# A two-layer trunk kernel: another order of token blocks in the mixers' last product, splits two blocks ahead, eight MLP pairs begun early, modulation slabs of two column blocks

## The chip, the cores and the metric

The kernel runs on one core of one Trainium2 chip. The metric is the time of one execution in device microseconds; the time shown is the median of several executions. The profiled execution is a single one with its own time. Engines are PE (matmul), PEld (its weight loads), DVE, ACT, POOL and SP, whose queue issues the DMAs.

## The reference

A batch of one sequence of 1024 tokens with 1024 features goes through two layers. Layer A has an mLSTM mixer, layer B multi-head latent attention; each is followed by an MLP with squared ReLU. A vector c gives shift, scale and gate for each part.

```python
for layer in range(DEPTH):                    # DEPTH = 2, layer 0 is A, layer 1 is B
    sh1, sc1, g1, sh2, sc2, g2 = split(silu(c) @ mod_w[layer] + mod_b[layer], 6)
    h = modulate(rms_norm(x, norm_g[layer, 0]), sh1, sc1)
    y = mlstm_mixer(h, ...) if layer == 0 else mla_mixer(h, ...)   # both end in "@ w_out"
    x = x + g1 * rms_norm(y, norm_g[layer, 1])
    h = modulate(rms_norm(x, norm_g[layer, 2]), sh2, sc2)
    y = square(relu(h @ ffn_w1[layer])) @ ffn_w2[layer]            # 1024 -> 4096 -> 1024
    x = x + g2 * rms_norm(y, norm_g[layer, 3])
```

`mlstm_mixer` projects h to q, k, v, an output gate and two scalar gates per head, runs a recurrence over chunks of 64 tokens, and multiplies the gated, normalised result by `w_out`. Everything is float32.

## The kernel before

**Matmuls.** Every operand is split into a rounded high half (a cast on ACT, L105, L438, L502, L546) and a low half (a subtraction on DVE, L106, L442, L504, L550). A product is three passes on PE: high by high (L155), low by high (L156) and high by low (L157). All engines work off their queues in order; the order within each queue is set by a scheduler when the kernel is built, from the program's order and its own costs. Work tiles come from a pool of 52 SBUF buffers (`U`), PSUM tiles from two of 1024 columns (`MM`) and four of 512 (`SM`).

**Start.** The first modulation (shift and scale of layer A) is needed as columns, one for each of 8 blocks k of 128 features. For each k a slab of `mod_w` (both column blocks of 128, all 1024 rows) is loaded in two tiles. DVE multiplies by the conditioning vector and adds over the 8 row blocks (`mod_sum`, L967 and L969, 8 operations of 128x256 for each k in two partial sums); POOL adds the two (L970); PE adds over the partitions by a matmul with a column of ones (`mod_col`, L976); DVE adds the bias (L978). Meanwhile ACT takes the sums of squares of the first four token blocks of x (L916), DVE the inverse roots (L164 to L172), ACT scales x (L920). `turned` transposes x on PE, ACT applies the modulation (L927) and casts, DVE makes the low half `hTl` (L106), and the projection of v and the gates (128x344 matmuls) follows for this k.

**Modulation of the rest.** `layer_mod(l, j)` is a list of steps: a DMA of 0.5 MB of `mod_w` (`modw`), a multiply-add of DVE (L263, L265) for each of 8 row blocks into `acc`, then transposes of `acc` on PE (L183) and a sum on DVE (L274). Other stages take steps from such lists: before, two after each of the last four blocks of v, six after each q or k head, and one after every third MLP product.

**End of a mixer.** For each token block, in the order `ORDER`, the gated result is turned and split (`gate_split` in layer A, `split` in layer B, one block ahead), multiplied by `w_out` (48 matmuls of 512 columns), normalised (ACT L178, DVE L164 to L172, L401, L402) and added to x (`mixer_out`). `h_norm` (L178, L492) prepares the MLP's input, `h_turn` transposes it (PE L183, ACT L457), `h_high` and `h_low` split it (L438, L442).

**MLP.** The up product of each of 16 pairs of column blocks is done in 7 products instead of 8. Products 1 and 2 need only the even token blocks; the other five need sums with the odd blocks (`odd_turn`, `odd_sums` L476 to L479, `odd_high`, `odd_low`). So `mlp_begin` starts with products 1 and 2 of the first `BEGUN` pairs. Their first weights come through `w_first` (DMA L499, ACT L502, DVE L504), the combined ones through `w_pair` (POOL L557 to L577, ACT L546, DVE L550). `up_product` adds each product to the pair's running sums (DVE L680, ACT L687, L683, L684).

Of the kernel before, what the change touches and what calls it, by code (L numbers as in the profile page):

```python
# [19 lines left out]
D = 1024  # L20
SEQ = 1024
P = 128
# [43 lines left out]
class Trunk:  # L66
# [356 lines left out]
    BEGUN = 6  # L423
# [204 lines left out]
    def mlp_begin(self, l, odd):  # L628
# [16 lines left out]
        up(2, 3, 5, 4)  # L645
        self.odd_turn(2, [odd.pop(5), odd.pop(7)])
        self.odd_low(0, "S1", "A22", "S4")
        up(3, 4, 5)
        self.odd_sums(2)
        self.w_step()  # L650
        up(4, 5)
        self.odd_high(2, "S2", "S3", "S1", "A22", "S4")
        self.odd_low(2, "S2", "S3")
        for _ in range(2):
            self.w_step()
        up(5)
        self.w_step()
        self.odd_low(2, "S1", "A22", "S4")
        self.w_step()

    def up_product(self, p, s):
# [7 lines left out]
        ps = st["ps"][:, (lo, hi)[s - 1]] if s in (1, 2) else self.SM()  # L669
# [49 lines left out]
    def mlp(self, l, done, extra, last=None):  # L719
# [43 lines left out]
        for p in range(NP):  # L763
            for o, s in enumerate((1, 2, 6, 7, 5, 4, 3)):
# [6 lines left out]
                if n % 3 == 0:  # L771
                    next(extra, None)
# [114 lines left out]
    def layer_a(self):  # L887
# [63 lines left out]
        def slab(k):  # L951

            w = T["mod_w"][0].rearrange("(i p) c -> p i c", p=P)
            us = [self.U("slab")[:, :D].rearrange("p (i s c) -> p i s c", i=4, s=2) for _ in range(2)]
            for j, u in enumerate(us):
                for s in range(2):
                    dma(out=u[:, :, s], in_=w[:, 4 * j : 4 * j + 4, s * D + k * P : s * D + (k + 1) * P])
            slabs.append([u.rearrange("p i s c -> p i (s c)") for u in us])

        def mod_sum(k):  # L960

            accs = [self.U("acc")[:, : 2 * P] for _ in range(2)]
            for i in range(KD):
                src, acc = slabs[k][i // 4][:, i % 4], accs[i % 2]
# [17 lines left out]
        def turned(k):  # L982

            ps = self.MM()
            mod_col(k, sums.pop(k), ps[:, 512:])
# [9 lines left out]
        load_xs(0, 2)  # L995
# [12 lines left out]
        turned(0)  # L1008
        for k in range(KD):
            if k < 4:  # L1010
                slab(k + 4)
            if k in (0, 2, 4):
# [819 lines left out]
```

## Time and profile before

| | |
|---|---|
| time, median of 3 executions | 2340.91 us (2340.1 to 2342.76) |
| profiled execution, its own time | 2336.43 us |
| its span from first to last instruction | 2334.7 us |
| mean granted clock of PE | 0.988 |
| busy: PE, PEld, DVE, ACT, POOL | 95%, 79%, 75%, 43%, 21% |

The own time is that of the execution which the rows below describe; the 1.7 us between it and the span lie before the first and after the last instruction. PE's share is an average: it is near 100% in most of the span and lower at the start (0 to 60 us), at about 100 to 110 us, and where a mixer passes into an MLP (464 to 645 us and 1610 to 1804 us). A granted clock of 1.00 stands for 2.4 GHz, one of 0.5 for 1.2 GHz.

### The profile page before, as it was taken

The page shows a single profiled execution, that of the slowest core. Times are in us where ns is not written, and L with a number is a line of the kernel's source. Part 1 is how long each engine was busy: PE and PEld are TensorE (multiplying, and loading weights), DVE is VectorE, ACT ScalarE, POOL GpSimd, SP SyncE. Part 2 cuts the span into 40 slices and gives each one's busy share as a digit, 9 for nine tenths or more (in the row PEclk, how much of TensorE's full clock was granted, in tenths as well). Part 3 has the DMA queues.
Part 4 walks back from the last instruction along what each step waited for, and adds up shares of the span by engine and source line. Part 5 has one row for each costly group of instructions (what it writes and reads, how often), then busy time and mean ns, then how long its engine had stood idle before and what let it go on. Part 6 is the DMA issues. An engine that isn't in the chain of part 4 may idle for free. (4 is left out here: it accounts for less than half of the span.)

```text
span 2334.7 us, 29139 instructions
## 1 busy us (share of the span) xinstructions
PE 2208.0 (95%) x10730; PEld 1833.8 (79%) x10730; DVE 1752.7 (75%) x2848; ACT 1007.7 (43%) x1637; POOL 480.7 (21%) x324
## 2 busy tenths in 40 slices
PE   5799999988999999999999999999889999999997
PEld 4798888866777777777798988987667888777776
DVE  6684676577888858788998676655777777588888
ACT  4421474563443464233344545544634444633321
POOL 1000110003433334231121000000034334333300
PEclk9999999999999999999999999999999999999999
DMA  9495343233665555454321000122346445544452
GB/s 272 142 322 201 100 73 99 91 109 127 221 226 189 190 180 160 119 167 146 102 88 44 17 17 15 46 73 81 109 156 220 152 149 189 172 131 140 142 174 99
DMA packets 304102, 318.09 MB, mean 136 GB/s; under 512 B 15976, under 2 KB 256216, under 8 KB 303960
## 3 DMA queue, kind: packets, MB, share of 16 engines
q1 hardware_dynamic: 303960, 316.23, 43.2%
q8 instruction: 84, 1.38, 0.2%
q14 instruction: 58, 0.48, 0.1%
HBM read 243.75 MB, written 72.43 MB: 135 GB/s over the span
## 5 line engine op out<-in xcount | busy, mean ns | idle before, releaser
L155 PE MATMUL mm<-whi,uh 128*128 128x512 f32 x688 | 273.1, 397 | 12.6 <-DVE y L760 10.7
L157 PE MATMUL mm<-whi,ul 128*128 128x512 f32 x688 | 271.2, 394 | 1.2 <-DVE ul L754 1.2
L156 PE MATMUL mm<-wlo,uh 128*128 128x512 f32 x688 | 271.1, 394 | 0.0
L577 POOL TENSOR_TENSOR tt<-raw,tt 128x512 f32<-128x512 f32 x60 | 118.0, 1967 | 668.7 <-DVE wlo L550 586.9
L760 DVE TENSOR_TENSOR y<-y,mm 128x1024 f32<-128x1024 f32 (+1 forms) x161 | 193.2, 1206 | 49.6 <-PE mm L157 49.4
L155 PE MATMUL sm<-hSh,whi 128*128 128x512 f32 x512 | 204.2, 399 | 11.3 <-DVE x L680 6.7
L157 PE MATMUL sm<-hSh,wlo 128*128 128x512 f32 x512 | 202.0, 396 | 2.2 <-DVE wlo L550 2.2
L156 PE MATMUL sm<-hSl,whi 128*128 128x512 f32 x512 | 202.5, 396 | 0.0
L550 DVE TENSOR_TENSOR wlo<-raw,whi 128x1024 fp32r<-128x1024 f32 x108 | 162.8, 1507 | 19.8 <-ACT whi L546 18.7
L754 DVE TENSOR_TENSOR ul<-u,uh 128x896 fp32r<-128x896 f32 (+1 forms) x120 | 151.0, 1289 | 32.0 <-ACT uh L748 24.4
L155 PEld LDWEIGHTS mm<-whi,uh 128*128 128x128 f32 x688 | 129.2, 188 | 49.2 <-DVE y L760 17.3
L680 DVE TENSOR_TENSOR x<-x,sm 128x512 f32<-128x512 f32 x192 | 127.8, 681 | 45.3 <-PE sm L157 41.9
L557 POOL TENSOR_TENSOR tt<-raw,raw 128x512 f32<-128x512 f32 x32 | 56.3, 1760 | 489.6 <-DVE hSl L442 461.5
L157 PEld LDWEIGHTS mm<-whi,ul 128*128 128x128 f32 x688 | 129.2, 188 | 32.4 <-DVE ul L754 2.1
L156 PEld LDWEIGHTS mm<-wlo,uh 128*128 128x128 f32 x688 | 129.2, 188 | 29.3
L748 ACT CAST uh<-u 128x896 fp32r<-128x896 f32 (+1 forms) x120 | 107.9, 945 | 84.8 <-PE mm L157 66.9
L265 DVE SCALAR_TENSOR_TENSOR acc<-modw,cact,acc 128x1024 f32<-128x1024 f32 x84 | 112.5, 1339 | 35.8 <-DMA modw<-in_mod_w_dram 29.1
L683 ACT ACTIVATE x<-x 128x1024 f32<-128x1024 f32 x64 | 67.7, 1058 | 155.2 <-DVE x L680 155.2
L582 ACT CAST w<-tt 128x512 fp32r<-128x512 f32 x60 | 37.2, 620 | 213.6 <-POOL tt L577 210.5
L155 PEld LDWEIGHTS sm<-hSh,whi 128*128 128x128 f32 x512 | 96.8, 189 | 37.9 <-DVE x L680 8.2
L546 ACT CAST whi<-raw 128x1024 fp32r<-128x1024 f32 x108 | 112.9, 1045 | 23.9 <-DVE wlo L550 10.2
L546 ACT CAST whi<-tt 128x1024 fp32r<-128x1024 f32 x60 | 62.9, 1048 | 136.9 <-issue 62.2
(404 smaller groups left out, 5991.7 us busy)
## 6 DMA issues: line engine op xcount, KB each, us to landing
raw<-in_ffn_w_dram SPq DMA_DIRECT2D x140, 512.0 KB
u<-us SPq DMA_DIRECT2D x112, 448.0 KB
us<-x SPq DMA_DIRECT2D x92, 512.0 KB
modw<-in_mod_w_dram SPq DMA_DIRECT2D x80, 512.0 KB
x<-xn SPq DMA_DIRECT2D x24, 512.0 KB
x<-x SPq DMA_DIRECT2D x24, 512.0 KB
x<-in_x_dram SPq DMA_DIRECT2D x16, 512.0 KB
slab<-in_mod_w_dram SPq DMA_DIRECT2D x32, 256.0 KB
```

What stands on the lines that cost most here:

```text
L155: mm(out, a[0], b[0], start=start, stop=False)
L156: mm(out, a[0], b[1], start=False, stop=False)
L157: mm(out, a[1], b[0], start=False, stop=stop)
L265: self.V.scalar_tensor_tensor(out=acc, in0=t, scalar=self.cact[:, k : k + 1], in1=acc, op0=ALU.mult, op1=ALU.add)
L546: S.copy(x[0], u)
L550: V.tensor_tensor(out=x[1], in0=u, in1=x[0].bitcast(F32), op=ALU.subtract)
L577: G.tensor_tensor(out=t1, in0=b21, in1=t2, op=ALU.subtract)
L680: V.tensor_tensor(out=dst, in0=src, in1=ps, op=ALU.add)
L683: S.activation(u, u, AF.Relu)
L748: S.copy(x[0], u)
L754: V.tensor_tensor(out=x[1], in0=u, in1=x[0].bitcast(F32), op=ALU.subtract)
L760: V.tensor_tensor(out=dst, in0=dst, in1=ps, op=ALU.add)
```

## The change

Five things are changed. The token blocks in both mixers' last product come in the order 0, 2, 4, 6, 1, 3, 5, 7. The turning and splitting of a block is issued two blocks ahead. Eight instead of six MLP pairs are begun, with `h_norm` for two blocks at a time, and two of the pairs (2 and 5) use `SM` tiles. The first modulation's slabs hold two column blocks (256 columns in one run of memory instead of 128), are all requested before other constants, and the sums for k = 0 and 1 are done by PE alone (L995, 8 matmuls of one column for each of shift and scale) instead of DVE, POOL and PE. `layer_mod(1, 2)` moves from the MLP of layer 0 to the end of the mixer's chunk loop, the steps after the blocks of v are dropped, q and k heads take seven instead of six, and MLP products two in five instead of one in three.

```diff
-    BEGUN = 6
+    BEGUN = 8
...
-    def h_norm(self, t):
-        x = self.mix[5].pop(t)
-        h = self.U("h")[:, :D]
-        self.S.activation(h, x, AF.Copy, scale=self.rms(x, D, h))
-        self.mix[6][t] = h
+    def h_norm(self, *ts):
+        xs = [self.mix[5].pop(t) for t in ts]
+        ssq = self.W("ssqs", [P, 4])
+        hs = [self.U("h")[:, :D] for _ in ts]
+        for i, (x, h) in enumerate(zip(xs, hs)):
+            self.S.activation(h, x, AF.Square, accum_out=ssq[:, i : i + 1])
+        r = self.rsqrt(ssq[:, : len(ts)], len(ts), 1.0 / D)
+        for i, (t, x, h) in enumerate(zip(ts, xs, hs)):
+            self.S.activation(h, x, AF.Copy, scale=r[:, i : i + 1])
+            self.mix[6][t] = h
...
-        up(0, 2, 4)
+        self.odd_sums(0)
+        up(0, 3, 4, 5)
+        self.h_norm(5, 7)
         self.odd_high(0, "S2", "S3")
-        self.h_norm(NT - 1)
-        up(1, 3)
-        self.w_step()
+        up(1, 4, 5, 6)
...
-            self.ups[p] = {"ps": self.MM(), "x": [self.U("x")[:, :1024], None]}
+            self.ups[p] = {"ps": None if p in (2, 5) else self.MM(), "x": [self.U("x")[:, :1024], None]}
...
-                if n % 3 == 0:
+                if n % 5 in (0, 2):
                     next(extra, None)
...
-            us = [self.U("slab")[:, :D].rearrange("p (i s c) -> p i s c", i=4, s=2) for _ in range(2)]
+            us = [self.U("slab")[:, :D].rearrange("p (i s c) -> p i s c", i=2, s=2) for _ in range(4)]
             for j, u in enumerate(us):
                 for s in range(2):
-                    dma(out=u[:, :, s], in_=w[:, 4 * j : 4 * j + 4, s * D + k * P : s * D + (k + 1) * P])
+                    dma(out=u[:, :, s], in_=w[:, 2 * j : 2 * j + 2, s * D + k * P : s * D + (k + 2) * P])
...
-                PE.matmul(ps[:, s : s + 1], acc[:, s * P : (s + 1) * P], self.ones[:, 0:1], start=True, stop=True)
+                if acc is not None:
+                    PE.matmul(ps[:, s : s + 1], acc[:, s], self.ones[:, 0:1], start=True, stop=True)
+                else:
+                    for i in range(KD):
+                        PE.matmul(ps[:, s : s + 1], slab_part(k, i)[:, s], self.cact[:, i : i + 1], start=i == 0, stop=i == KD - 1)
...
-        load_xs(2, 4)
+        for g in range(3):
+            slab(2 * g)
+            self._raw()
+        slab(6)
         normed(xs[:4], True)
-        slab(0)
-        self._raw()
-        mod_sum(0)
-        for k in range(1, 4):
-            slab(k)
-        for k in range(1, 4):
+        for k in range(2, 4):
             mod_sum(k)
...
-            for _ in range(2):
-                next(mods, None)
...
-                for _ in range(6):
+                for _ in range(7):
                     next(mods, None)
...
+        mods = self.layer_mod(1, 2)
+        self.early = 1
...
+                if j >= 2:
+                    next(mods, None)
+        finish(mods)
...
-    ORDER = (0, 1, 2, 3, 4, 6, 5, 7)
+    ORDER = (0, 2, 4, 6, 1, 3, 5, 7)
...
-        if n in (4, 6):
-            self.h_even(n - 4, [hs.pop(t) for t in ((0, 2) if n == 4 else (4, 6))])
-        elif n == 5:
+        if n in (3, 5):
+            j = n - 3
+            self.h_even(j, [hs.pop(t) for t in (2 * j, 2 * j + 2)])
+        elif n == NT - 1:
             self.odd_turn(0, [hs.pop(1), hs.pop(3)])
...
-        for p in {4: (0, 1), 5: (0, 2), 6: (0, 1, 3), 7: (1, 2)}.get(n, ()):
-            next(self.first[p], None)
+        for p in range(self.BEGUN):
+            if 0 <= n - 3 - p < 3:
+                next(self.first[p], None)
```

Three places show how instructions move. The first is DVE's queue at the start of the program. Before, the sums of the first slab (`acc_151`, `acc_152`) stand among the steps of the inverse root for x (`rst`, `rsy`):

```order
L170 TENSOR_TENSOR rst_126<-rsy_125,rsv_124 128x4
L171 TENSOR_TENSOR rst_126<-rst_126,rsy_125 128x4
L967 TENSOR_SCALAR acc_151<-slab_142,cact 128x256
L967 TENSOR_SCALAR acc_152<-slab_142,cact 128x256
L172 SCALAR_TENSOR_TENSOR rsy_125<-rst_126,rsy_125 128x4
L969 SCALAR_TENSOR_TENSOR acc_151<-slab_142,cact,acc_151 128x256
L969 SCALAR_TENSOR_TENSOR acc_152<-slab_142,cact,acc_152 128x256
L170 TENSOR_TENSOR rst_126<-rsy_125,rsv_124 128x4
L969 SCALAR_TENSOR_TENSOR acc_151<-slab_143,cact,acc_151 128x256
L969 SCALAR_TENSOR_TENSOR acc_152<-slab_143,cact,acc_152 128x256
L171 TENSOR_TENSOR rst_126<-rst_126,rsy_125 128x4
```

In the changed kernel DVE's queue after its first four small operations is this; `mm_219` and `mm_262` are PE's sums for k = 0 and 1, `acc_199` and `acc_209` DVE's for k = 2 and 3:

```order
L997 TENSOR_TENSOR modcol<-mm_219,bcols 128x2
L999 SCALAR_TENSOR_TENSOR modcol<-modcol,gcols 128x1
L982 TENSOR_SCALAR acc_199<-slab_130,cact 128x256 x2
L982 TENSOR_SCALAR acc_209<-slab_130,cact 128x256 x2
L984 SCALAR_TENSOR_TENSOR acc_199<-slab_131,cact,acc_199 128x256 x2
L984 SCALAR_TENSOR_TENSOR acc_209<-slab_131,cact,acc_209 128x256 x2
L997 TENSOR_TENSOR modcol<-mm_262,bcols 128x2
L984 SCALAR_TENSOR_TENSOR acc_199<-slab_132,cact,acc_199 128x256 x2
L984 SCALAR_TENSOR_TENSOR acc_209<-slab_132,cact,acc_209 128x256 x2
L999 SCALAR_TENSOR_TENSOR modcol<-modcol,gcols 128x1
L984 SCALAR_TENSOR_TENSOR acc_199<-slab_133,cact,acc_199 128x256 x2
L164 TENSOR_SCALAR rsv_181<-ssqs_172 128x4
```

DVE now takes PE's sum for k = 0 first, then 16 sums of the second slab, with PE's sum for k = 1 between them; the inverse root of x (from L164) starts at the last of these, where it began ahead of all sums before.

The second place is PE's queue in the first q head, where the columns of the next modulation are turned (`acc`, L183). Before, these two rows stand 27 rows behind the transpose of the positions (`posf`):

```order
L155 MATMUL sm_1012<-whi_552,hTh_785 128x344
L156 MATMUL sm_1012<-wlo_553,hTh_785 128x344
L157 MATMUL sm_1012<-whi_552,hTl_786 128x344
L183 MATMUL sm_1039<-ident,acc_855 128x128 x4
L183 MATMUL sm_1045<-ident,acc_855 128x128 x4
L155 MATMUL sm_1075<-whi_544,hTh_698 128x344
```

In the changed kernel the same place in the q head holds only a transpose of the gates, 75 rows behind `posf`:

```order
L156 MATMUL sm_1080<-wlo_553,hTh_785 128x344
L157 MATMUL sm_1080<-whi_552,hTl_786 128x344
L1211 MATMUL sm_1113<-ident,gate_1023 1x32
L155 MATMUL sm_1123<-whi_544,hTh_698 128x344
L156 MATMUL sm_1123<-wlo_545,hTh_698 128x344
```

and the turning of `acc` stands 164 rows behind `posf`:

```order
L155 MATMUL sm_1186<-whi_813,hTh_463 128x344
L156 MATMUL sm_1186<-wlo_814,hTh_463 128x344
L157 MATMUL sm_1186<-whi_813,hTl_464 128x344
L183 MATMUL sm_1213<-ident,acc_1014 128x128 x4
L183 MATMUL sm_1219<-ident,acc_1014 128x128 x4
L155 MATMUL sm_1225<-whi_801,hTh_243 128x344
L156 MATMUL sm_1225<-wlo_802,hTh_243 128x344
```

The turning of `acc` has moved back by 137 rows of PE's queue, and a small transpose for the gates, which DVE and ACT compute, now comes ahead of it.

The third place is ACT's queue at the end of layer A's mixer. `mm_4298` is the product of the last block but one; its sum of squares (L178) stands behind six of the eight copies of turned MLP input (L457, each row x2):

```order
L105 CAST aTh_4279<-gt_4281 128x512 x2
L492 ACTIVATE h_4259<-xn_4236,rsy_4263 128x1024
L457 ACTIVATE hr_4347<-sm_4348,modcol 128x256 x2
L457 ACTIVATE hr_4347<-sm_4355,modcol 128x256 x2
L457 ACTIVATE hr_4362<-sm_4363,modcol 128x256 x2
L178 ACTIVATE xn_4387,ssq_4388<-mm_4298 128x1024
L457 ACTIVATE hr_4362<-sm_4370,modcol 128x256 x2
L438 CAST hSh_4067<-hr_4347 128x2x256
```

In the changed kernel the sum of squares of the last block but one (`mm_4321`) and the work of `h_norm` (L497) stand ahead of the copies, and that of the last block (`mm_4395`) behind three of four:

```order
L507 CAST whi_4316<-raw_4167 128x1024
L178 ACTIVATE xn_4372,ssq_4373<-mm_4321 128x1024
L507 CAST whi_4390<-raw_4319 128x1024
L497 ACTIVATE h_4295<-xn_4147,rsy_4300 128x1024
L497 ACTIVATE h_4296<-xn_4277,rsy_4300 128x1024
L457 ACTIVATE hr_4444<-sm_4445,modcol 128x256 x2
L457 ACTIVATE hr_4444<-sm_4452,modcol 128x256 x2
L457 ACTIVATE hr_4459<-sm_4460,modcol 128x256 x2
L178 ACTIVATE xn_4474,ssq_4475<-mm_4395 128x1024
L507 CAST whi_4492<-raw_4393 128x1024
```

## Rows read from the trace of the kernel before

**Rows 1.** Windows: stretch, then busy us (x instructions) per engine, granted clock, DMA, GB/s.

```profile
0.00:60.00 60.00, 33.06 (x163) 29.15 (x163) 40.10 (x116) 26.83 (x37) 11.50 (x28) 0.97 0.93 265
290.00:464.00 174.00, 173.73 (x894) 146.57 (x893) 114.40 (x303) 96.89 (x213) 8.18 (x8) 1.00 0.33 84
464.00:561.00 97.00, 83.08 (x348) 64.43 (x347) 69.55 (x117) 51.66 (x84) 15.86 (x10) 0.93 0.37 108
561.00:645.00 84.00, 78.74 (x337) 61.66 (x336) 69.66 (x82) 38.32 (x40) 38.54 (x23) 1.00 0.63 208
1610.00:1725.00 115.00, 98.74 (x419) 77.64 (x418) 80.72 (x148) 64.97 (x108) 18.48 (x11) 0.94 0.35 103
1725.00:1804.00 79.00, 73.20 (x307) 57.27 (x306) 64.93 (x77) 36.20 (x38) 35.42 (x21) 0.98 0.66 215
1856.00:1914.00 58.00, 58.00 (x252) 46.98 (x251) 42.92 (x46) 25.15 (x27) 21.32 (x12) 1.00 0.45 148
```

**Rows 2.** PE in order of time, start: start us, us, line, operation, count.

```profile
18.64 1.01 PE L976 MATMUL mm<-ones,acc 128*128 128x1 f32 x4 [11.07 <-POOL acc L970]
...
31.23 1.50 PE L155 MATMUL sm<-whi,hTh 128*128 128x344 f32 x4
...
54.09 0.50 PE L976 MATMUL mm<-ones,acc 128*128 128x1 f32 x4
...
58.70 0.78 PE L157 MATMUL sm<-whi,hTl 128*128 128x344 f32 x4
```

**Rows 3.** DVE in order of time, start.

```profile
11.49 0.16 DVE L171 TENSOR_TENSOR rst<-rst,rsy 128x4 f32<-128x4 f32 x1
```

**Rows 4.** DVE groups, 0 to 60 us: count, busy us, mean ns, idle before.

```profile
L969 DVE SCALAR_TENSOR_TENSOR acc<-slab,cact,acc 128x256 f32<-128x256 f32 x48 | 21.8, 493 | 1.0 <-DVE rst L170 0.7 <-DMA slab<-in_mod_w_dram 0.3
L967 DVE TENSOR_SCALAR acc<-slab,cact 128x256 f32<-128x256 f32 x16 | 6.4, 433 | 3.7 <-DMA slab<-in_mod_w_dram 3.7
L106 DVE TENSOR_TENSOR hTl<-t,hTh 128x512 fp32r<-128x512 f32 x8 | 5.4, 680 | 4.0 <-ACT hTh L105 4.0
```

**Rows 5.** ACT in order of time, start.

```profile
9.70 1.06 ACT L916 ACTIVATE h<-x 128x1024 f32<-128x1024 f32 x1 [0.15 <-DMA x<-in_x_dram]
...
17.95 4.26 ACT L920 ACTIVATE x<-x,rsy 128x1024 f32<-128x1024 f32 x4 [7.10 <-DVE rsy L172]
...
23.59 0.62 ACT L105 CAST hTh<-t 128x512 fp32r<-128x512 f32 x1
```

**Rows 6.** DMA view, 8 to 45 us.

```profile
DMA packets 19893, 10.79 MB, mean 292 GB/s; under 512 B 1906, under 2 KB 19818, under 8 KB 19892
```

**Rows 7.** PE in order of time, 99 to 113 us.

```profile
110.47 1.94 PE L183 MATMUL sm<-ident,acc 128*128 128x128 f32 x8 [10.55 <-DVE acc L265]
...
112.78 0.49 PE L157 MATMUL sm<-whi,hTl 128*128 128x344 f32 x1
```

**Rows 8.** DVE in order of time, 99 to 113 us.

```profile
99.09 0.33 DVE L1169 TENSOR_SCALAR gate<-sm,gbias 32x128 f32<-32x128 f32 x1
...
112.79 0.27 DVE L1179 SCALAR_TENSOR_TENSOR gate<-gate 32x128 f32<-32x128 f32 x1
```

**Rows 9.** Waits of PE, 464 to 561 us: total, times, longest.

```profile
PE mm L157 <- DVE wlo L504: 4.2, 2, 2.2
PE mm L155 <- DVE xn L401: 3.4, 1, 3.4
```

**Rows 10.** ACT in order of time, 485 to 489 us.

```profile
485.14 2.84 ACT L457 ACTIVATE hr<-sm,modcol 128x256 f32<-128x256 f32 x6 [5.14 <-PE sm L183]
487.85 1.05 ACT L178 ACTIVATE xn<-mm 128x1024 f32<-128x1024 f32 x1
```

**Rows 11.** DVE groups, 464 to 645 us: count, busy us, mean ns, idle before.

```profile
L680 DVE TENSOR_TENSOR x<-x,sm 128x512 f32<-128x512 f32 x36 | 23.9, 678 | 8.8 <-PE sm L157 8.6
...
L504 DVE TENSOR_TENSOR wlo<-raw,whi 128x1024 fp32r<-128x1024 f32 x6 | 7.3, 1217 | 0.6 <-ACT whi L502 0.6
...
L442 DVE TENSOR_TENSOR hSl<-hs,hSh 128x512 fp32r<-128x512 f32 x8 | 5.1, 682 | 0.0
```

More of the change, by code (lines that the diff above doesn't have):

```diff
@@ L666, in up_product @@
         if p not in self.ups:
-            self.ups[p] = {"ps": self.MM(), "x": [self.U("x")[:, :1024], None]}
+            self.ups[p] = {"ps": None if p in (2, 5) else self.MM(), "x": [self.U("x")[:, :1024], None]}
         st = self.ups[p]
-        ps = st["ps"][:, (lo, hi)[s - 1]] if s in (1, 2) else self.SM()
+        ps = st["ps"][:, (lo, hi)[s - 1]] if s in (1, 2) and st["ps"] is not None else self.SM()
         w = self.w_take((0, p), s)
@@ L953, in slab, with slab_part @@
             w = T["mod_w"][0].rearrange("(i p) c -> p i c", p=P)
-            us = [self.U("slab")[:, :D].rearrange("p (i s c) -> p i s c", i=4, s=2) for _ in range(2)]
+            us = [self.U("slab")[:, :D].rearrange("p (i s c) -> p i s c", i=2, s=2) for _ in range(4)]
             for j, u in enumerate(us):
                 for s in range(2):
-                    dma(out=u[:, :, s], in_=w[:, 4 * j : 4 * j + 4, s * D + k * P : s * D + (k + 1) * P])
-            slabs.append([u.rearrange("p i s c -> p i (s c)") for u in us])
+                    dma(out=u[:, :, s], in_=w[:, 2 * j : 2 * j + 2, s * D + k * P : s * D + (k + 2) * P])
+            slabs.append(us)
+        def slab_part(k, i):
+            return slabs[k // 2][i // 2][:, i % 2, :, (k % 2) * P : (k % 2 + 1) * P]
         def mod_sum(k):
-            accs = [self.U("acc")[:, : 2 * P] for _ in range(2)]
+            u = self.U("acc")
+            accs = [u[:, o : o + 2 * P].rearrange("p (s c) -> p s c", s=2) for o in (0, 2 * P)]
             for i in range(KD):
-                src, acc = slabs[k][i // 4][:, i % 4], accs[i % 2]
+                src, acc = slab_part(k, i), accs[i % 2]
                 c = self.cact[:, i : i + 1]
@@ L984, in turned @@
             ps = self.MM()
-            mod_col(k, sums.pop(k), ps[:, 512:])
+            mod_col(k, sums.pop(k, None), ps[:, 512:])
             self.transposes(ps, [x[:, k * P : (k + 1) * P] for x in xs[:4]])
@@ L1009, in layer_a @@
         for k in range(KD):
-            if k < 4:
-                slab(k + 4)
-            if k in (0, 2, 4):
-                for _ in range(3 if k == 4 else 1):
-                    self._raw()
-            if k >= 6:
-                load_xs(2 * k - 8, 2 * k - 6)
+            if 1 <= k < 4:
+                self._raw()
+            if k >= 4:
+                load_xs(k, k + 1)
             if k == KD - 1:
@@ L1106, in layer_a @@
                 V.tensor_scalar(out=dst, in0=dst, scalar1=self.headg[:, j : j + 1], scalar2=None, op0=ALU.mult)
+                if j >= 2:
+                    next(mods, None)
+        finish(mods)
         del hT
         order = self.ORDER
-        aT = self.gate_split(0, hn[0], sg)
+        pre = deque(self.gate_split(t, hn[t], sg) for t in order[:2])
         self.mixer_start(0, x_in, "x1")
@@ L1141, in mixer_out @@
         self.dma(out=x_out[tb * P : (tb + 1) * P, :], in_=xn)
-        if n == 5:
-            self.odd_sums(0)
-        for t in {2: (0, 1), 3: (2,), 4: (3, 4), 5: (6,), 6: (5,)}.get(n, ()):
-            self.h_norm(t)
-        for p in {4: (0, 1), 5: (0, 2), 6: (0, 1, 3), 7: (1, 2)}.get(n, ()):
-            next(self.first[p], None)
+        if n in (1, 3, 5):
+            self.h_norm(*self.ORDER[n - 1 : n + 1])
+        for p in range(self.BEGUN):
+            if 0 <= n - 3 - p < 3:
+                next(self.first[p], None)
         if n == NT - 1:
```

39 lines of the change are left out of this document (22 added, 17 removed).

## The prediction

> **What bounds the kernel now.** I first read the page, then busy time by stretch, then PE's waits and the order in time where PE stands. In a steady MLP stretch PE takes 58.00 of 58 us for 252 matmuls of 512 columns, 0.230 us each [rows 1]. Nothing that only frees DVE, ACT or DMA is worth anything there. PE is short of work in four places. From 0 to 60 us it is busy for 33.06 us. At 99.9 us it stops for 10.55 us before the turning of `acc`, because DVE has not finished it [rows 7]. From 464 to 561 us (mixer A to MLP) it is busy for 83.08 of 97 us at a mean clock of 0.93, and from 1610 to 1725 us (mixer B to MLP) for 98.74 of 115 us at 0.94 [rows 1]. The begun pairs that follow lose 84.00 - 78.74 = 5.3 us and 79.00 - 73.20 = 5.8 us. The chunk phase of layer A (290 to 464 us) loses 0.3 us. The change touches all of these.
>
> **The start: +6 us, between 0 and +9.** Before, this stage ends at 59.5 us, after the last projection matmuls [rows 2]. DVE is idle for slabs only 3.7 + 0.3 us in all [rows 4], so wider slabs cannot give back more than that here. What decides is the new order of DVE's queue. The loads come at the rate of before, as a cautious value: the fourth x block is there at 9.70 us [rows 5], and 2.1 MB at 292 GB/s [rows 6] take 7.2 us, so the pair is complete at about 17, its first tile at about 11.
> PE's own sums are 2 x 16 matmuls, and a matmul of one column leaves two records: four records take 1.01 us at 18.64 and 0.50 us at 54.09 [rows 2]. At 0.25 us per record 64 records take 16 us. In PE's order 46 of them come until k = 0 is complete, so k = 0 is ready at 11 + 11.5 = 22.5 us and k = 1 at 27. DVE's queue holds the bias addition for k = 0 ahead of its 16 sums for k = 2 and 3, and that for k = 1 in their middle. A sum costs (21.8 + 6.4) / 64 = 0.44 us [rows 4], so the first eight end at 26.5, the wait for k = 1 at 27.2, the second eight at 31. The inverse root of x, 11 steps of about 0.2 us [rows 3], stands at their end and is done at about 33. Before, it was done at 17.95, when ACT began to scale x for 4.26 us [rows 5]. Scaling, transposes, modulation and cast (the cast 0.62 us) bring the first projection matmul to 39 or 40 us instead of 31.23 [rows 2]. At that point DVE has the same left in both kernels: 32 sums (14 us), seven or eight `hTl` of 0.68 us [rows 4], three weight halves. Before, 28.3 us passed from there to the end of the stage; here no slab is waited for any more and PE has been at work for longer, for which I take off 2 us. The stage ends near 66 us: +6.
> If PE gets its full clock during its own sums, k = 0 is there at 17 and DVE is held by the second pair's landing at about 24 instead; the inverse root ends near 28, the stage near 60: 0. If nothing is taken off, +9. I choose the half clock, because PE's four records at 18.64, which follow an idle PE like these, ran at it.
> The Trainium skill ("TensorE: Matmul & The Clock Gate", section "Back-to-back issue gap") lists a gap of about 60 cycles, some 25 ns at full clock, for a matmul of 1 to 64 columns. By that figure the 64 records would take 1.6 us, the sums would be ready when the slab has landed, and the start would cost 0, so that the sum below would be -29 and the time 2312. The trace does not agree: 0.125 us at the full clock and 0.25 us at the lower one [rows 2]; the same section says that the table leaves the weight load out.
>
> **The stop at 99.9 us: -11 us, between -8 and -12.** It costs 10.55 us, and behind it 344-column matmuls run at the half clock still at 112.78 [rows 7], about 1.5 us more. The turning of `acc` moves from 27 to 164 rows of PE's queue behind `posf`, that is by about 24 us of PE work. DVE was not idle in the stop: it worked off eight multiply-adds, the rope tables and the gates. The same work is now hidden behind the q head. What is late next is the transpose of the gates, 75 rows (12 us) behind `posf`, a chain of small steps of DVE and ACT. Before, DVE's steps of it run from 99.09 to 112.79 us with all eight multiply-adds among them [rows 8]; now three stand among them, but all rope steps ahead of them, so I put its end some 13 us behind `posf`: 1.3 us of wait, at most 4. The later turnings have seven steps per head for the eight steps that the v blocks no longer take, and come no nearer to their data than before.
>
> **Modulation in the chunk phase: +1 us, between 0 and +4.** Eight loads of 0.5 MB and eight multiply-adds, some 11 us of DVE in all. DVE is busy for 114.40 of 174 us and DMA for 0.33 there [rows 1], so they are covered; two small groups of transposes come onto PE. Without cover it would be up to 4 us of waits.
>
> **Mixer A to MLP: -12 us, between -4 and -17.** PE idles 97 - 83.08 = 13.9 us [rows 1], and the half clock behind the stops costs about 5 more (0.07 x 97 = 6.8, less the idle part): 19. The largest waits are for the low halves of the first MLP weights (4.2 us) and for `xn` (3.4 us) [rows 9]. The latter is an order fault: the sum of squares of the last block but one starts only at 487.85, behind six copies that had waited 5.14 us for PE's transposes [rows 10]. In the new ACT order it stands ahead of the copies. Splits two blocks ahead take away the wait for `aTh`. And PE has more to do before it needs an odd block: from the last output product on 16 early products (192 matmuls, 44 us) and 32 transposes (3.5 us), 48 us, instead of 12 (144) and 32, 37 us. DVE needs until then 20 low halves of 0.68, about 8 of 1.22, eight odd sums of the same length, 6 additions of 0.68 [rows 11] and two inverse roots, about 43 us in all. So PE becomes the longer of the two by 5 us, where DVE was by about 3 before. What remains are short waits in this order: PSUM tiles that an addition frees while it stands behind an odd sum (about 1.2, 1.0 and 3.2 us) and `h_norm`'s last scaling (0.7): 7 us. 19 - 7 = 12. The lower bound is the case that the backlog of DVE is worked off in the same order as before (only `xn` and `aTh` go), the upper that nothing but 2 us remains.
>
> **Mixer B to MLP: -13 us, between -6 and -18.** The same mechanism: 115 - 98.74 = 16.3 us idle [rows 1] and about 5 for the clock, 21; 8 remain.
>
> **Begun pairs: +3 us in each layer, between 0 and +6.** The six of before lose about 1 us each [rows 1], and there are two more; modulation steps come at 2 in 5 instead of 1 in 3 products. A pair has 5 late products, 60 x 0.230 = 13.8 us of PE, against 69.66 / 6 = 11.6 us of DVE [rows 1], now about 12.
>
> **The sum.** 6 - 11 + 1 - 12 + 3 - 13 + 3 = -23 us against the profiled execution's own 2336.4, so 2313.4. The median of the runs shown stands 4.5 us above that execution, so 2318 is the time I give.
>
> **Rivals.**
> (1) PE's sums run at the full clock and the start costs nothing: -29, time 2312. Against it the half clock at 18.64 [rows 2].
> (2) The mixers give half, because DVE falls behind at the odd sums: -6 and -6.5 instead of -12 and -13, time 2330. For it: 43 us of DVE against 48 of PE is a thin margin, and two more pairs' low halves are in it. Against it: the largest single waits come from order, not from load.
> (3) The gates' transpose takes over most of the stop, because DVE does rope work ahead of the gates: -4 instead of -11, time 2325.
> (4) Slower: DVE becomes the bound in the 16 begun pairs. Place: from the first odd product of each layer to the last begun pair. If low halves and multiply-adds bring DVE from 12 to 17 us for a pair, against 13.8 of PE, each pair loses 3 us, 48 in all in place of the 6 above: -29 + 48 = +19, time 2360. It decides from 29 / 16 = 1.8 us lost per pair, 15.6 us of DVE. For it: DVE is busy for 69.66 of 84 us and POOL for 38.54 there [rows 1]; against it: some 3.5 us more per pair are needed.
>
> **Chances.** My forecast 0.48, (1) 0.14, (2) 0.20, (3) 0.06, (4) 0.12. Of (2) 0.02 and of (4) 0.05 would end within 0.2% of before, the other 0.07 of (4) above it. 0.2% is 4.7 us, about what a measurement of this kernel can tell from no change. Faster by more than that 0.86, within it 0.07, slower 0.07. The range of the likeliest alone is 2305 to 2326; to leave out no more than 2 in 10, with the bounds of the start and the mixers and the cases (1) to (3), it goes from 2298 to 2334.
>
> **What the profile would show.** Right: the first projection matmul at 36 to 40 us, DVE idle ahead of L997 until PE's sums end; no stop over 3 us near 100 us; in the stretches behind both mixers PE short by 7 to 9 us rather than 14 to 16, with L178 of the last block but one directly behind its product; DVE near 12 us per begun pair. Wrong: PE's sums done before 20 us; waits for L476 to L479 or L442 of more than 10 us behind a mixer; PE standing for weights (L555) in every begun pair.

## The result, and the profile after

The changed kernel takes 2318.87 us (median of 4, 2316.33 to 2319.99) against 2341.84 us (2340.1 to 2344.94): a ratio of 0.9899, 95% interval 0.9882 to 0.9916, 23 us faster. Its profiled execution took 2319.99 us over a span of 2318.2 us, 16.4 us less than the profiled one of before, which was below its own median. Beside some of the experiments the same kernel was timed again, for the comparison with them:

> The changed kernel once more, unchanged, beside the next three on one chip, as their measure. Every theory expects the ratio of before, 0.990, some 2314 to 2319 us.

It took 2317.64 us, 0.9907 (0.9892 to 0.9923). A ratio is always that to the kernel before, timed beside the run on the same chip; its medians beside the experiments were 2337.67, 2338.48 and 2338.22 us.

I cut both spans at six places that every version has, by the start of the row named; the change is spread over them very unevenly.

| from, to | before | after | difference | forecast |
|---|---|---|---|---|
| start, transpose of the positions (`posf`) | 95.3 | 109.9 | +14.6 | +6 |
| to the first product with `w_out` of layer A | 291.9 | 292.5 | +0.6 | -11 and +1 |
| to the first down product of MLP A | 448.9 | 435.9 | -13.0 | -12 and +3 |
| to the first product with `w_out` of layer B | 714.4 | 714.6 | +0.2 | 0 |
| to the first down product of MLP B | 442.3 | 423.6 | -18.7 | -13 and +3 |
| to the last matmul | 331.3 | 331.5 | +0.2 | 0 |

The windows that answer to [rows 1], with the same columns, of the changed kernel:

```profile
0.00:60.00 60.00, 38.46 (x168) 35.28 (x169) 29.93 (x86) 20.11 (x28) 9.01 (x26) 0.93 0.80 265
290.00:464.00 174.00, 168.44 (x862) 142.69 (x861) 127.80 (x294) 102.18 (x221) 14.45 (x10) 0.98 0.33 98
464.00:561.00 97.00, 90.39 (x408) 72.70 (x407) 67.73 (x131) 57.70 (x97) 12.88 (x7) 0.98 0.42 121
561.00:645.00 84.00, 81.54 (x352) 64.56 (x352) 73.47 (x84) 34.92 (x37) 35.28 (x23) 1.00 0.70 224
1590.00:1705.00 115.00, 108.10 (x487) 87.17 (x486) 76.69 (x153) 65.37 (x114) 11.58 (x7) 0.97 0.35 104
1705.00:1804.00 99.00, 97.20 (x422) 77.75 (x421) 84.41 (x99) 44.37 (x46) 42.86 (x27) 1.00 0.68 223
```

PE is short by 97 - 90.39 = 6.6 us behind mixer A and by 115 - 108.10 = 6.9 us behind mixer B, where it was 13.9 and 16.3; windows moved along with the last product with `w_out` give the same. The chunk phase (290 to 464 us) was full before and now lacks 5.6 us.

The start, PE in order of time, answering to [rows 2]:

```profile
10.93 13.79 PE L995 MATMUL mm<-cact,slab 128*128 128x1 f32 x64 [0.16 <-DMA slab<-in_mod_w_dram]
32.42 0.69 PE L183 MATMUL mm<-ident,x 128*128 128x128 f32 x2 [7.70 <-ACT x L930]
...
39.10 1.50 PE L155 MATMUL sm<-whi,hTh 128*128 128x344 f32 x4
...
49.59 0.61 PE L992 MATMUL mm<-ones,acc 128*128 128x1 f32 x4 [1.24 <-POOL acc L985]
...
57.87 0.49 PE L156 MATMUL sm<-wlo,hTh 128*128 128x344 f32 x1
...
68.41 0.90 PE L157 MATMUL sm<-whi,hTl 128*128 128x344 f32 x4
73.16 0.31 PE L183 MATMUL sm<-ident,rows 32*128 32x32 f32 x1 [3.85 <-DVE rsy L165]
```

PE's own sums (L995) take 13.79 us; then PE stands for 7.7 us until x is scaled. The first projection matmul comes at 39.10 us (31.23 before), the stage ends at 69.3 us (59.5), and PE stands again for 3.85 us behind it. In between PE waits 1.24 us for sums of DVE and POOL, and the granted clock is 0.63 from 50 to 55 us and 0.50 from 55 to 60 us (0.91 from 50 to 60 us before): a 344-column matmul then takes 0.49 us instead of 0.32. DVE and ACT of the same stretch show why the stage starts late, answering to [rows 3, 5]:

```profile
10.80 0.26 DVE L223 COPY bcols<-sm 128x96 f32<-128x96 f32 x1
20.92 0.16 DVE L997 TENSOR_TENSOR modcol<-mm,bcols 128x2 f32<-128x2 f32 x1 [9.86 <-PE mm L995]
...
27.32 0.16 DVE L164 TENSOR_SCALAR rsv<-ssqs 128x4 f32<-128x4 f32 x1
...
30.96 0.16 DVE L172 SCALAR_TENSOR_TENSOR rsy<-rst,rsy 128x4 f32<-128x4 f32 x1
37.27 0.21 DVE L1347 CAST posf<-posi 8x128 f32<-8x128 int32 x1 [6.15 <-DMA posi<-in_positions_dram]
...
39.62 1.13 DVE L982 TENSOR_SCALAR acc<-slab,cact 128x256 f32<-128x256 f32 x4
```

```profile
31.22 4.27 ACT L930 ACTIVATE x<-x,rsy 128x1024 f32<-128x1024 f32 x4 [20.25 <-DVE rsy L172]
...
68.47 1.05 ACT L926 ACTIVATE h<-x 128x1024 f32<-128x1024 f32 x1
...
71.60 1.04 ACT L926 ACTIVATE h<-x 128x1024 f32<-128x1024 f32 x1
...
72.64 1.67 ACT L920 COPY vext<-sm 128x256 f32<-128x256 f32 x8
```

DVE does nothing from 11 to 20.92 us, because the bias addition for k = 0 stands first in its queue. The inverse root of x ends behind the sums, at 31.1, and ACT scales x at 31.22 instead of 17.95. At 68.47 ACT takes the sums of squares of the second half of x, four of them, until 72.6, ahead of the copies of v that free the PSUM tiles. (The view puts PE's 3.85 us down to `rsy` of DVE, which ended last; in the run with late x below PE waits for the copies.)

The DVE rows show one more wait. From 31.1 to 37.27 us DVE stands for the positions (`posi`): their load is requested at 32.6 us, behind all slabs, where it was requested at 4.3 us before. Behind that cast in DVE's queue stand the sums for k = 4 to 7, which then run without a wait for a slab (39.62).

At the place of [rows 7], PE waits only for the gates; near 400 us a stop is new:

```profile
124.70 0.18 PE L1211 MATMUL sm<-ident,gate 32*1 32x32 f32 x1 [2.67 <-DVE gate L1202]
...
392.91 0.28 PE L157 MATMUL sm<-mh,ml 128*128 128x258 f32 x1
393.98 1.97 PE L183 MATMUL sm<-ident,hn 128*128 128x128 f32 x16 [0.78 <-ACT num L1309]
400.72 1.97 PE L183 MATMUL sm<-ident,hn 128*128 128x128 f32 x8 [4.78 <-DVE gt L1338]
```

Before, the same transposes came without a wait, directly behind matmuls of the output gate's projection:

```profile
385.07 2.34 PE L183 MATMUL sm<-ident,hn 128*128 128x128 f32 x20
```

Behind mixer A (464 to 561 us), this is what is left of the waits of PE that answer to [rows 9] (us in all, times, longest):

```profile
PE mm L155 <- DVE x L690: 6.4, 3, 4.8
```

The wait for `xn` and that for the low halves of the first weights are gone. What remains is three waits for additions, the longest 4.8 us.

### The profile page after: what moved, and what is told of

Same layout as the page of the kernel before. It is cut to its first block, busy times and chain, and to the rows that moved or that the text cites. A ratio compares the mean times of both kernels' runs of the same rounds, so it can differ in the third digit from the quotient of the medians.

```text
span 2318.2 us, 29189 instructions
## 1 busy us (share of the span) xinstructions
PE 2217.4 (96%) x10786; PEld 1851.1 (80%) x10786; DVE 1745.9 (75%) x2792; ACT 1012.0 (44%) x1641; POOL 472.0 (20%) x322
## 5 line engine op out<-in xcount | busy, mean ns | idle before, releaser
L582 POOL TENSOR_TENSOR tt<-raw,tt 128x512 f32<-128x512 f32 x60 | 112.4, 1873 | 632.6 <-DVE wlo L555 632.6
L155 PE MATMUL sm<-hSh,whi 128*128 128x512 f32 x544 | 216.2, 397 | 8.2 <-DVE x L690 7.9
L156 PE MATMUL sm<-hSl,whi 128*128 128x512 f32 x544 | 214.9, 395 | 0.0
L157 PE MATMUL sm<-hSh,wlo 128*128 128x512 f32 x544 | 213.8, 395 | 0.3 <-DVE wlo L555 0.3
L555 DVE TENSOR_TENSOR wlo<-raw,whi 128x1024 fp32r<-128x1024 f32 x104 | 157.0, 1510 | 17.9 <-ACT whi L551 17.8
L758 ACT CAST uh<-u 128x896 fp32r<-128x896 f32 (+1 forms) x120 | 108.0, 946 | 84.9 <-PE mm L157 66.8
L155 PEld LDWEIGHTS sm<-hSh,whi 128*128 128x128 f32 x544 | 102.5, 188 | 35.4 <-DVE x L690 6.6
L265 DVE SCALAR_TENSOR_TENSOR acc<-modw,cact,acc 128x1024 f32<-128x1024 f32 x84 | 117.3, 1397 | 9.4 <-DMA modw<-in_kv_mod_w_dram 5.8
L551 ACT CAST whi<-tt 128x1024 fp32r<-128x1024 f32 x60 | 62.9, 1048 | 139.1 <-issue 62.2
L157 PEld LDWEIGHTS sm<-hSh,wlo 128*128 128x128 f32 x544 | 102.6, 189 | 25.2 <-DVE wlo L555 1.0
```

The costliest lines, as they stand in the source:

```text
L155: mm(out, a[0], b[0], start=start, stop=False)
L156: mm(out, a[0], b[1], start=False, stop=False)
L157: mm(out, a[1], b[0], start=False, stop=stop)
L265: self.V.scalar_tensor_tensor(out=acc, in0=t, scalar=self.cact[:, k : k + 1], in1=acc, op0=ALU.mult, op1=ALU.add)
L551: S.copy(x[0], u)
L555: V.tensor_tensor(out=x[1], in0=u, in1=x[0].bitcast(F32), op=ALU.subtract)
```

## The experiments

**PE's sums or the rest of the start.** The first kernel has the whole start of before in the changed kernel (slabs, sums and every load; the cut shows the order of the loads):

```diff
-        load_xs(0, 4)
+        load_xs(0, 2)
...
+        load_xs(2, 4)
         normed(xs[:4], True)
-        for k in range(2, 4):
+        slab(0)
+        self._raw()
+        mod_sum(0)
+        for k in range(1, 4):
+            slab(k)
+        for k in range(1, 4):
             mod_sum(k)
```

> The changed kernel with the start of the kernel before (slabs of one column block, all first sums on DVE, loads in the old order); all else as changed. In the trace of the changed kernel the first projection stage ends at 69.3 us (59.5 before), and PE stands again for 3.9 us until 73.2 behind it and then runs at the half clock until 78.6. My theory: these are a loss that nothing later takes back, so the time falls by 10 to 15 us, to 2304 to 2309 us. Rival: what follows waits for DVE and DMA anyway and takes the delay up, so the time stays within 3 us of 2319.

2309.31 us (2305.57 to 2310.47), 0.9877 (0.9857 to 0.9897). `posf` comes at 97.1 us instead of 109.9, which is more than the 10 us by which its span (2308.0) is shorter. Timed, it is 8 us below the changed kernel's second timing and 0.3 us outside what the theory expected. That timing was on another chip, and the intervals of the two ratios overlap; the pair of kernels at the end of this section, timed on one chip, shows clear of noise that the start's loss is not taken up later.

**Only the early loads of x undone.**

```diff
-            if k >= 4:
-                load_xs(k, k + 1)
+            if k >= 6:
+                load_xs(2 * k - 8, 2 * k - 6)
```

> The changed kernel with the loads of token blocks 4 to 7 of x where they stood before (two each at k = 6 and 7). Theory: because these blocks arrive early, ACT takes their four sums of squares ahead of the copies of v that free the PSUM tiles, and PE stands for 3.9 us near 70 us and loses about 3 us more to the half clock; with late loads two blocks' copies of v stand ahead, so 3 to 7 us come back: 2312 to 2316 us. Rival: ACT is behind with the casts of weights there in any case, and the time stays at 2319.

2313.91 us (2310.64 to 2315.51), 0.9899 (0.9879 to 0.9919). The end of the first stage in this kernel, on PE:

```profile
65.10 0.79 PE L157 MATMUL sm<-whi,hTl 128*128 128x344 f32 x4
66.64 0.24 PE L183 MATMUL sm<-ident,rows 32*128 32x32 f32 x1 [0.75 <-ACT vext L920]
67.05 0.43 PE L155 MATMUL sm<-whi,hTh 128*128 128x344 f32 x1 [0.16 <-ACT vext L920]
```

PE goes on after 0.75 us where it stood for 3.85 us, and `posf` comes at 101.6 us. So of the 14.6 us that the start loses, 8.3 are not in this kernel: some 5 are the stop with the half clock behind it, and 3.4 lie ahead of it (the stage ends at 65.9 us instead of 69.3), about as much as the start varies between executions of the same code. The other 6.3 us are in the rest of the start. The timed gain is 3.7 us between medians, as forecast by the theory, but the ratio does not differ from the changed kernel's.

**Wide slabs without PE's sums.** This kernel has late x, `layer_mod(1, 2)` early (below), and

```diff
-        for k in range(2, 4):
+        for k in range(4):
             mod_sum(k)
```

> The kernel with late x and layer_mod(1, 2) at j = 0 to 2, and slabs of two column blocks as changed, but the sums for k = 0 and 1 on DVE as before: the width of the slabs without PE's sums. Theory: DVE waited only 4 us for slabs before, so width alone cannot gain more than that, and in this order of DVE's queue the inverse root of x still ends behind the sums of the second slab pair: the first projection stage ends at 60 to 64 us, the time is 2303 to 2308 us, not better than with the whole start of before (2303). Rival: the wide slabs shorten the start: stage end at 56 or less, time under 2300.

2315.06 us (2314.5 to 2316.69), 0.9902 (0.9888 to 0.9916); 7 us above what the theory allowed. DVE and ACT in it:

```profile
10.85 1.14 DVE L982 TENSOR_SCALAR acc<-slab,cact 128x256 f32<-128x256 f32 x4 [0.46 <-DMA slab<-in_mod_w_dram]
18.25 0.88 DVE L982 TENSOR_SCALAR acc<-slab,cact 128x256 f32<-128x256 f32 x3 [6.25 <-DMA slab<-in_mod_w_dram]
...
24.05 0.16 DVE L164 TENSOR_SCALAR rsv<-ssqs 128x4 f32<-128x4 f32 x1
...
32.53 0.16 DVE L172 SCALAR_TENSOR_TENSOR rsy<-rst,rsy 128x4 f32<-128x4 f32 x1
```

```profile
32.80 4.26 ACT L930 ACTIVATE x<-x,rsy 128x1024 f32<-128x1024 f32 x4 [22.52 <-DVE rsy L172]
```

DVE has its first sums at 10.85, but waits 6.25 us for the second slab pair, and the inverse root ends behind the sums of both pairs; x is scaled at 32.80, still later than with PE's sums, and the stage ends at 68.6, not at 60 to 64. So PE's sums alone are not what costs the start. What both kernels share is the place of the inverse root in DVE's queue, behind sums that need the second slab pair, and DVE's wait for `posi` (5.4 us here). That these cost the start is read from the queues; neither was moved alone.

**The stop near 400 us.** The modulation that had moved into the chunk loop goes back into the MLP:

```diff
-        mods = self.layer_mod(1, 2)
-        self.early = 1
...
-                if j >= 2:
-                    next(mods, None)
-        finish(mods)
...
-        extra = [... for js in ((4, 3), (5,))]
+        extra = [... for js in ((2, 4, 3), (5,))]
```

> The changed kernel with layer_mod(1, 2) back in the MLP of layer 0. In the changed kernel PE's queue has only 4 matmuls of the output gate's projection behind the last chunk (48 before), and PE stands for 4.8 us near 400 us and then runs at the half clock. Theory: the moved steps have shifted that projection ahead of the chunk, and it no longer covers the last chunk's chain on ACT and DVE; with the steps back, 48 matmuls stand there, and 6 to 9 us come back, less 1 for the steps in the MLP: 2311 to 2314 us. Rival: the stop comes from the two splits ahead of the mixer, and the time stays at 2319.

2322.8 us (2320.47 to 2324.25), 0.9936 (0.9919 to 0.9953): 5 us slower, not faster. The stop is gone, and the stretch from the first chunk product to the first product with `w_out` falls from 129.5 to 121.5 us. But the stretch from the last product of mixer A to the first down product grows from 337.3 to 346.5 us. PE's waits there, from 640 to 840 us, first of this kernel, then of the changed one:

```profile
PE sm L155 <- DVE x L690: 7.8, 5, 3.7
PE mm L155 <- ACT x L697: 2.0, 1, 2.0
```

```profile
PE sm L155 <- DVE x L690: 4.9, 3, 3.7
```

The mechanism was right and the price of the other side wrong: eight more loads with their multiply-adds in that MLP, at two steps in five products, cost 9 us, not 1.

**The same modulation at the front of the chunk loop.**

```diff
-                if j >= 2:
+                if j < 3:
                     next(mods, None)
```

> The changed kernel, but layer_mod(1, 2) takes its steps at j = 0 to 2 of the chunk loop instead of from j = 2 on. The scheduler then leaves 44 matmuls of the output gate's projection behind the last chunk instead of 4. Theory: the stop of 4.8 us near 400 us and the half clock behind it go, the MLP keeps its gain: 6 to 9 us faster than the changed kernel of the same chip. Rival (putting the steps anywhere in the chunk loop costs DVE what the MLP gains): within 2 us of it.

2317.83 us (2317.13 to 2319.99), 0.9912 (0.9898 to 0.9925), the same as the changed kernel's 2317.64. In the trace the stop is gone and that stretch is 125.7 us instead of 129.4, but 2.9 us come back in the mixer and the MLP behind it. The rival holds in the time; half of the loss is still there.

**One block ahead instead of two.**

```diff
-        pre = deque(self.gate_split(t, hn[t], sg) for t in order[:2])
+        pre = deque([self.gate_split(order[0], hn[order[0]], sg)])
...
-            if n + 2 < NT:
-                pre.append(self.gate_split(order[n + 2], hn[order[n + 2]], sg))
+            if n + 1 < NT:
+                pre.append(self.gate_split(order[n + 1], hn[order[n + 1]], sg))
```

(and the same in layer B)

> The changed kernel with the turning and splitting one block ahead instead of two, in both mixers. Theory: the waits for the high half (1.1 us in layer A, 2.6 in layer B before) come back with their half clock, the stop near 400 us stays: 3 to 6 us slower than the changed kernel, 2322 to 2325 us. Rival (the stop near 400 us comes from the second split ahead of the mixer): that stop of 4.8 us goes, and the time is 2314 to 2319.

2317.58 us (2317.33 to 2319.05), 0.9916 (0.99 to 0.9933), like the changed kernel. Both theories missed: the stop near 400 us stays (4.8 us), and the waits for the high half come back only once, with 0.6 us. Between the first and the last product with `w_out` 1.5 us are lost in each layer. With the even blocks first, the second split ahead is worth next to nothing.

**The mixers' end of before.** Order, one block ahead, `h_norm`, six pairs and `mlp_begin` of before; start and modulation as changed.

> The changed kernel with the mixers' end of the kernel before: its order of token blocks, one block ahead, h_norm of one block, six begun pairs and the old order in mlp_begin; start and modulation as changed. Theory: the order, the two blocks ahead and the longer run of early products are what gains; by the traces the stretch from the last product of mixer B to the first down product fell by 18.7 us and that of mixer A by 13, part of which is the moved modulation. So 22 to 30 us are lost: 2337 to 2349 us, as slow as before or slower. Rival: the gain comes from the modulation steps that left the MLP, and the mixers' order is worth less than 10: under 2328 us.

2336.55 us (2332.87 to 2338.87), 0.9992 (0.9983 to 1.0001): 19 us slower than the changed kernel on the same chip, somewhat less than the theory expected (22 to 30). The new end of the mixers as a whole is worth 19 us. But MLP B still gains without them: from the last product of mixer B to the first down product it takes 329.9 us, against 339.6 in the kernel before.

**Six pairs in the new order.**

```diff
-    BEGUN = 8
+    BEGUN = 6
...
-        up(1, 4, 5, 6)
+        up(1, 4, 5)
```

(and so on: every `up` without pairs 6 and 7)

> The changed kernel with six instead of eight pairs begun, order and splits as changed. Theory: two pairs are 11 us of PE work that cover DVE's backlog of some 43 us at the odd sums; without them PE has 37 us there and waits 4 to 6 us more in each layer: 2325 to 2331 us. Rival: the order of blocks and h_norm of two blocks do it alone: 2316 to 2320.

2333.77 us (2330.87 to 2335.29), 0.9982 (0.9972 to 0.9991): 16 us slower, above the 2325 to 2331 us that were expected. PE's waits from 1640 to 2000 us, and ACT at the first of the like waits in layer A:

```profile
PE sm L155 <- ACT whi L551: 8.6, 4, 4.5
PE sm L157 <- DVE wlo L555: 2.2, 2, 1.4
PE mm L155 <- DVE x L686: 1.8, 2, 1.0
```

```profile
540.67 1.14 ACT L438 CAST hSh<-hr 128x512 fp32r<-128x512 f32 x2 [1.09 <-DVE hr L478]
543.61 1.14 ACT L438 CAST hSh<-hr 128x512 fp32r<-128x512 f32 x2 [1.79 <-DVE hr L479]
544.65 1.04 ACT L551 CAST whi<-tt 128x1024 fp32r<-128x1024 f32 x1
```

PE waits for the first combined weight (`whi`, L551). Its cast stands in ACT's queue behind the casts of the odd sums, which wait for DVE. So DVE's backlog is what the two more pairs cover, and it reaches PE by way of ACT.

**The density of the modulation steps.** One line, in the changed kernel and the other way round in the kernel before:

```diff
-                if n % 5 in (0, 2):
+                if n % 3 == 0:
```

> The changed kernel with one line as before: modulation steps after every third MLP product instead of two in five. With the mixers of before (the run above) the stretch from the last product of mixer B to the first down product still fell from 339.6 to 329.9 us, and in it stood only this line. Theory: the density of steps decides it, since it shifts what DVE and the weights' DMA do in the begun pairs: 6 to 12 us slower, 2324 to 2330 us. Rival: that fall has another cause (the scheduler's order around the odd sums), and the time stays within 3 us of 2318.

> The kernel before with one line of the change: modulation steps after two in five MLP products. Theory (density decides): 6 to 12 us faster than before, 2327 to 2333 us. Rival: within 3 us of before.

The changed kernel with every third: 2331.29 us (2328.7 to 2333.4), 0.9971 (0.996 to 0.9982), 14 us slower. The kernel before with two in five: 2325.3 us (2324.11 to 2328.09), 0.9947 (0.9934 to 0.9959), 12 or 13 us faster by this line alone. Both are a little more than the 6 to 12 us expected. DVE's waits in the begun pairs of layer B, first of the kernel before (1725 to 1804 us), then of the changed kernel with every third product (1710 to 1810 us), then of the kernel before with two in five (1715 to 1795 us):

```profile
DVE acc L265 <- DMA modw<-in_mod_w_dram: 10.7, 5, 4.1
DVE x L711 <- ACT x L684: 2.6, 2, 1.6
```

```profile
DVE acc L265 <- DMA modw<-in_mod_w_dram: 9.8, 5, 5.0
DVE x L690 <- PE sm L157: 7.9, 5, 2.1
```

```profile
DVE x L711 <- ACT x L684: 4.0, 2, 2.9
DVE x L680 <- PE sm L157: 3.5, 3, 2.1
DVE w L584 <- ACT w L582: 0.6, 1, 0.6
```

With every third, DVE stands for 10 us before multiply-adds whose `modw` has not landed; with two in five, no such wait is left. Why the load is late is read from SP's queue. In the kernel before, SP's own waits in the same stretch (1715 to 1804 us) are led by a store that waits for DVE (L713):

```profile
SPq L713 <- DVE x L712: 21.9, 5, 6.5
```

and a `modw` load stands behind such stores, in the order of SP (source line, transfer):

```
L260 DMA modw_15475<-in_mod_w_dram 128x1024
L713 DMA us_2_14805<-x_15463 128x1024
L535 DMA raw_15496<-in_ffn_w_dram 128x8x128
L716 DMA us_2_14805<-x_15464 128x1024
L535 DMA raw_15498<-in_ffn_w_dram 128x8x128
L260 DMA modw_15540<-in_mod_w_dram 128x1024
```

With two in five, seven `modw` loads of this stretch stand ahead of that store instead of six:

```
L709 DMA us_2_14805<-x_15397 128x512
L260 DMA modw_15478<-in_mod_w_dram 128x1024
L535 DMA raw_15499<-in_ffn_w_dram 128x8x128
L713 DMA us_2_14805<-x_15466 128x1024
L535 DMA raw_15501<-in_ffn_w_dram 128x8x128
L716 DMA us_2_14805<-x_15467 128x1024
L260 DMA modw_15522<-in_mod_w_dram 128x1024
```

So by the order DVE waited for a load that waited, in SP's queue, for a result of DVE. That two in five takes the waits away is shown; that it does so by this place in the queue alone was not tried apart.

Cut by layer, the profiled executions show where that line acts. The columns are the two stretches from the first product with `w_out` to the first down product:

| kernel | layer A | layer B |
|---|---|---|
| before | 448.9 | 442.3 |
| before, two in five | 448.6 | 431.9 |
| changed | 435.9 | 423.6 |
| changed, every third | 439.1 | 430.7 |
| changed, six pairs | 439.6 | 430.7 |
| changed, mixers' end of before | 441.2 | 435.1 |
| changed, `layer_mod(1, 2)` in MLP A | 445.8 | 422.9 |

In the kernel before, two in five is worth 10.4 us in layer B and nothing in layer A. PE gains in the begun pairs of layer A too (82.74 busy of 88 us from 561 us, against 86.24 from 562 us), but loses it again in the rest of that MLP (650 to 836 us, first before, then with two in five):

```profile
PE sm L155 <- DVE x L680: 2.7, 3, 1.2
```

```profile
PE sm L155 <- DVE x L680: 7.1, 3, 3.6
```

MLP A has the steps of three modulations to take there and MLP B those of one. So the 9 us that `layer_mod(1, 2)` gives by leaving MLP A are in part a loss that the denser steps bring into it; how large a part was not tried.

**The parts that gain, together.** The start of before and the early `layer_mod(1, 2)` in the changed kernel:

> The kernel of the start before together with layer_mod(1, 2) at j = 0 to 2: every part of the change that gains, without the two places that lose. Theory: the two losses are apart from each other and add up, 10 for the start and 8 for the stop near 400 us: 15 to 20 us faster than the changed kernel of the same chip, about 2300 us. Rival (the start is partly taken up by later waits when the stop is gone): 8 to 12 us.

2302.95 us (2300.96 to 2305.14), 0.9847 (0.9833 to 0.986), 14.7 us faster than the changed kernel on the same chip and the fastest of all. `posf` comes at 95.0 us. That is more than the rival's 8 to 12 us, and 0.3 us short of the 15 to 20 that the theory expected of two losses that add up. This kernel and the one with the same modulation at the front of the chunk loop differ by the start alone and were timed on the same chip: 2302.95 against 2317.83 us, with intervals of the ratio far apart. So the start costs 14.9 us of the time; `posf` differs by 13.0 us between the two (95.0 and 108.0).

## Why the prediction was right

The time, 2318, and the sign were right. The terms were not all: the start and the chunk phase lost more than forecast, the moved and the denser modulation steps gained where nothing or a loss was forecast, and these cancelled. That the time came out within 1 us is luck: the sum was made from the profiled execution of before, and the two profiled executions differ by 16 us, not by 23; the other 7 us are the place of each among its runs.

**The start** was a loss, as forecast, and the chain of steps holds to within 2 us up to the first projection matmul: k = 0 at 20.92 (22.5 forecast), inverse root at 31.1 (33), first projection matmul at 39.10 (39 or 40). The choice of the half clock was right: 64 records took 13.79 us, not 8. (0.25 us per record was a little too much: it spread the end of the last of four records over all four.) The step that was mis-sized is "take off 2 us": 30.2 us passed from there, 2 more than before instead of 2 less. No slab was waited for, as said, but the sum put DVE's wait for `posi`, 6.15 us with sums standing behind it, at nothing, and so PE's wait for such sums at 49.59 us and the half clock that follows. This chain is read from the rows; no run requested `posi` earlier. And one step was missing: that the early loads of x put four sums of squares ahead of the copies of v. Together +14.6, above the bound of +9.

**The stop at 99.9 us** went as forecast: 10.55 us became one wait of 2.7 us for the gates (1.3 forecast, at most 4), and the half clock behind it is gone: about -9.

**The modulation in the chunk phase** was the step that failed. I wrote that the steps "are covered" there, since DVE and DMA had room. They are, but the scheduler placed the output gate's projection earlier, and that projection was the cover of the last chunk's chain on ACT and DVE. The stop of 4.8 us with its half clock cost 8 us by the run with the steps moved back; +1 was forecast, at most 4. The same run showed what the move gives: 9 us in the MLP, in part against the denser steps there, which the forecast didn't have at all.

**The mixers**: the waits that I listed went, and the rest of 7 us behind each was right (6.6 and 6.9). That PE's longer run of early products covers DVE's backlog is shown by the run with six pairs, which loses 16 us. But the -13.0 us of layer A, beside a forecast of -12 and +3, are not all the mixer's: with `layer_mod(1, 2)` back in the MLP the stretch falls by 3.1 us only. My reason for the splits two ahead is not borne out: one ahead does as well.

**The begun pairs** had the wrong sign. I charged +3 in each layer for denser steps and two more pairs, by DVE's load; the runs with one line show the denser steps to be worth 12 to 14 us in all, most of it in layer B. What I didn't read was DVE's own waits in the begun pairs: 10.7 us for `modw` stood in the trace of before, between PE's small waits.

Rival (1), the full clock, fell in the rows of L995. Rival (2), half the gain in the mixers, fell in the waits (6.6 and 6.9 us remain, as forecast), but the run with the mixers' end of before gives it 19 us of the forecast 25, by the stretches above 5.3 in layer A and 11.5 in layer B: denser steps alone take some of the same waits. Rival (3) happened in a small way, 2.7 us. Rival (4) is opposite to what the begun pairs did: DVE's busy time there rose, and PE waited less.

**What stays open.** The runs' gains do not add: the mixers' end (19), two more pairs (16) and denser steps (12 to 14) overlap, since each covers the same waits. Why the early `layer_mod(1, 2)` gained nothing with the new start and some 6 us with that of before (2302.95 against 2309.31, on two chips) was not tried apart. Within the start, the inverse root's place and the late load of `posi` remain two causes that no run separates. One execution's start also moves by some 3 us with the place at which a half-clock stretch falls: the same start code put `posf` at 109.9, 109.7 and 107.2 us in three kernels.

## What to carry to other kernels

Read the waits of every engine that feeds the bound one, not only of that one: 10 us of DVE waiting for a load at the head of its queue showed on PE as eight waits of at most 1.5 us, and a change of one number in how often a load is issued removed them. When work is moved into a stage "with room", look at what a scheduler then puts elsewhere, for the filler behind the last item of that stage may be what it takes. And a load that is requested late holds up all that stands behind its first use in a queue, however small it is: look for the operation at the head of each queue, and for what it waits for. And a sum taken off one engine frees nothing while its result stands first in that engine's queue: DVE stood for 9.86 us here.

## What the runs showed of the hardware

A matmul of one column with a 128x128 operand leaves two records. At the lower clock (1.2 GHz) four records took 1.01 us [rows 2] and the 64 of L995 13.79 us, so that each further record took (13.79 - 1.01) / 60 = 0.213 us; at the full 2.4 GHz four took 0.50 us [rows 2]. Thirteen microseconds of such matmuls did not raise the clock: behind them PE paused for 7.7 us, and the 344-column matmuls after 39 us still came at the pace of the lower clock. This is read from the pace of the records, since the column of the granted clock stands at 1.00 in that stretch (11 to 25 us).

The loads of the start moved at 353 GB/s from 11 to 32 us with slabs in runs of 1 KB, against 292 GB/s with runs of 512 B [rows 6]. It was worth nothing to this start, whose stage ended 9.8 us later.
